# Huber loss on one core: sixteen rows of the first loads sent apart, and new widths for the second and the end tiles

## The chip, the cores and the metric

The kernel runs on one core of a Trainium2 chip. The metric is the device time of one execution in microseconds (us). The time before is the median of three runs. A profile of one execution shows the instructions of each engine and the packets of the sixteen DMA engines that serve the core; VectorE is called DVE in it, ScalarE ACT, SyncE SP.

## The reference

```
diff = pred - target                      # both 8192 x 8192, float32
abs_diff = |diff|
out = 0.5 * diff**2          where abs_diff <= 1
      abs_diff - 0.5         elsewhere
```

Two inputs of 268 MB are read from the chip's memory (HBM) and one output of 268 MB is written.

## The kernel before, in words

The arrays are taken as flat. The 524,288 columns that each of the 128 partitions gets are cut into 37 tiles (`widths`, line 28). A tile is one contiguous stretch of HBM; each partition takes one contiguous run of it, so a load or store of a tile has 128 rows, one per partition. Tile 0 has GAP = 9408 columns, tile 1 has 12,000, tiles 2 to 35 have W = 14,592 each, and the last has 6752.

All of it lives in one buffer `mem` of 3 W + GAP columns. Even and odd tiles alternate between places. `at_b(i)` is where a tile's target is loaded, where the difference is written over it and where the result ends: column 0 for even tiles, W for odd ones. `at_a(i)` is where its pred is loaded, later used for a temporary: 2 W for even tiles, flush to the buffer's end for odd ones. The pred places of neighbouring full tiles overlap by R = W - GAP = 5184 columns; `covered(i)` gives this overlap. Tile i's work does that stretch first (the held piece), so that the next tile's pred can be loaded over it early.

`parts(i)` says in which column ranges a tile is loaded: tile 0 and the last two come in halves, the third from the end in two unequal parts, all others in one. `load(i)` issues for each part the pred and then the target (for the last tile both preds first). All loads and stores are issued by SyncE on one queue, in program order: line 80 in `load`, line 85 in `store`.

`work(i, then)` cuts the parts into pieces (`pieces`, `split`) and runs three steps over each: `subtract` (line 95, DVE: d = a - b; line 96, ACT: absolute value), `square` (line 100, DVE: clip; line 103, ACT: 0.5 x squared) and `combine` (line 107, DVE: the larger of |d| - 0.5 and the square). After the held piece's subtract it calls `then`, which issues the next tile's load.

The order of SyncE's queue is: load(0), load(1), then for each tile store(i - 1), and inside the work of tile i load(i + 1). A pred load waits on the subtract of the held piece that it overwrites. A target load waits on the store of the tile two before, which held its place. A store waits on the last combine of its tile. The waits follow from the data and are put in by the framework.

Of the kernel before, what the change touches and what calls it, by code (L numbers as in the profile page):

```python
# [1 line left out]

# [4 lines left out]


@with_exitstack
def kernel(  # L10
    ctx: ExitStack,
    tc: tile.TileContext,
    pred: bass.AP,
    target: bass.AP,
    out: bass.AP,
):
    nc = tc.nc
    P = 128
    fp32 = mybir.dt.float32
    Alu = mybir.AluOpType  # L20
    Act = mybir.ActivationFunctionType
    SQRT_HALF = 0.70710678118654752

    total = pred.shape[0] * pred.shape[1] // P
    W = 14592
    GAP = 9408
    R = W - GAP
    widths = [GAP, W - R // 2] + [W] * 34
    widths.append(total - sum(widths))
    n = len(widths)  # L30
    starts = [sum(widths[:i]) * P for i in range(n)]

    def block(x, i):
        flat = x.rearrange("r m -> (r m)")
        return flat[starts[i] : starts[i] + P * widths[i]].rearrange("(p m) -> p m", p=P)

    pool = ctx.enter_context(tc.tile_pool(name="memory", bufs=1))
    mem = pool.tile([P, 3 * W + GAP], fp32, name="mem")

    def at_a(i):
        return 3 * W + GAP - widths[i] if i % 2 else 2 * W

    def at_b(i):
        return W if i % 2 else 0

    def covered(i):  # L50

        if i + 1 >= n:
            return (0, 0)
        lo = max(at_a(i), at_a(i + 1))
        hi = min(at_a(i) + widths[i], at_a(i + 1) + widths[i + 1])
        return (lo - at_a(i), hi - at_a(i)) if hi > lo else (0, 0)


    def parts(i):
        w = widths[i]  # L60
        if i == n - 3:
            return [(w - 2 * R, w), (0, w - 2 * R)]
        if i in (0, n - 2, n - 1):
            return halves(w)
        return [(0, w)]

    def halves(w):
        h = w // 32 * 16
        return [(0, h), (h, w)]

    def view(base, lo, hi):
        return mem[:, base + lo : base + hi]

    def load(i):
        order = [(x, part) for part in parts(i) for x in "pt"]
        if i == n - 1:
            order = [(x, part) for x in "pt" for part in parts(i)]
        for x, (lo, hi) in order:
            src, base = (pred, at_a(i)) if x == "p" else (target, at_b(i))
            nc.sync.dma_start(out=view(base, lo, hi), in_=block(src, i)[:, lo:hi])  # L80

    def store(i):
        w = widths[i]
        for lo, hi in halves(w) if i == n - 1 else [(0, w)]:
            nc.sync.dma_start(out=block(out, i)[:, lo:hi], in_=view(at_b(i), lo, hi))

    def split(lo, hi, size):
        k = -((lo - hi) // size)
        edges = [lo + (hi - lo) * j // k // 16 * 16 for j in range(k)] + [hi]
        return list(zip(edges[:-1], edges[1:]))  # L90


    def subtract(i, lo, hi, at):
        a, d = view(at_a(i), lo, hi), view(at_b(i), lo, hi)
        nc.vector.tensor_tensor(out=d, in0=a, in1=d, op=Alu.subtract)  # L95
        nc.scalar.activation(out=d, in_=d, func=Act.Abs)  # L96

    def square(i, lo, hi, at):
        d, t = view(at_b(i), lo, hi), view(at_a(i) + at, 0, hi - lo)
        nc.vector.tensor_scalar(  # L100
            out=t, in0=d, scalar1=-1.0, scalar2=1.0, op0=Alu.max, op1=Alu.min
        )
        nc.scalar.activation(out=t, in_=t, func=Act.Square, scale=SQRT_HALF)  # L103

    def combine(i, lo, hi, at):
        d, t = view(at_b(i), lo, hi), view(at_a(i) + at, 0, hi - lo)
        nc.vector.scalar_tensor_tensor(  # L107
            out=d, in0=d, scalar=-0.5, in1=t, op0=Alu.add, op1=Alu.max
        )

    def pieces(i, lo, hi):


        c0, c1 = covered(i)
        c0, c1 = max(lo, c0), min(hi, c1)
        if c1 <= c0:
            k = -((lo - hi) // (R // 2 if i < n - 1 else R // 4))
            return [], [(i, x, y, x) for x, y in split(lo, hi, -((lo - hi) // k))]
        x, y = (lo, c0) if c0 > lo else (c1, hi)
        m = max(c1 - c0, (y - x) // 32 * 16)  # L120
        rest = [(x, x + m), (x + m, y)] if y > x + m else [(x, y)]
        return [(i, c0, c1, x)], [(i, x, y, x) for x, y in rest]

    def work(i, then):

        todo, held = [], []
        for part in parts(i):
            first, rest = pieces(i, *part)
            todo += first + rest
            held += first  # L130
        mid, end = [], []
        if held:
            subtract(*todo.pop(0))
        then()
        while todo or mid or end or held:
            if todo:
                piece = todo.pop(0)
                subtract(*piece)
                mid.append(piece)
                if len(mid) < 2 and todo:  # L140
                    continue
            if mid:
                piece = mid.pop(0)
                square(*piece)
                end.append(piece)
                if len(end) < 2 and (todo or mid):
                    continue
            combine(*end.pop(0))
            mid += held
            held = []  # L150

    ctx.enter_context(tc.manual_schedule())

    load(0)
    load(1)
    for i in range(n):
        if i > 0:
            store(i - 1)
        work(i, lambda: load(i + 1) if 0 < i < n - 1 else None)
    store(n - 1)  # L160


# [1 line left out]
_INS = ['pred', 'target']  # L164
_OUTS = [((8192, 8192), 'float32')]


# [23 lines left out]
```

## Time and profile before

| What | Value |
|---|---|
| Median of three runs | 1867.21 us (1866.58 to 1867.41) |
| The profiled execution | 1866.7 us |
| Its span, first to last instruction | 1864.9 us |
| DVE busy | 1408.3 us, 76% |
| ACT busy | 912.5 us, 49% |
| Queue of the loads and stores, share of 16 DMA engines | 99.9% |
| HBM read and written | 536.87 MB and 268.44 MB, 432 GB/s over the span |

The page gives each engine's busy time, the packets and bytes of the DMA queues, the costliest groups of instructions and the time from a transfer's issue to its landing. A transfer is spread over several DMA engines and has landed when each of them has set its mark. DMA share is the mean busy share of the sixteen DMA engines; a packet is put into the window in which it starts, so very short windows can show more than 1.

### The profile page before, as it was taken

The numbers are of one execution on the slowest core, as the hardware profiler recorded it, in microseconds if no ns is written. First come the engines' busy times: TensorE is split into PE (matmuls) and PEld (weight loads), VectorE is DVE, ScalarE is ACT, GpSimd is POOL, SyncE is SP. The second block draws the span as 40 slices with busy tenths as digits, with TensorE's granted clock in tenths as the row PEclk, the third lists the DMA queues.
The fourth block names the chain that finished last, engine by engine and source line by source line (L and its number), as shares of the span: only waits on it lengthen the run. The fifth ranks groups of instructions, "written<-read, shape, count | busy, mean of one in ns | idle before, by whom it ended". The sixth has DMA issues, their size and how long they took to land.

```text
span 1864.9 us, 960 instructions
## 1 busy us (share of the span) xinstructions
DVE 1408.3 (76%) x357; ACT 912.5 (49%) x239; POOL 0.2 (0%) x4
## 2 busy tenths in 40 slices
DVE  5677777777788777777778877777777887777986
ACT  3455444444555545444455554544445555454554
POOL 0000000000000000000000000000000000000000
DMA  9999999999999999999999999999999999999999
GB/s 421 418 436 431 436 431 432 437 427 436 438 428 434 439 428 435 438 429 433 438 428 436 438 428 435 438 428 436 438 427 437 436 429 437 435 429 436 428 437 393
DMA packets 17287, 805.37 MB, mean 432 GB/s; under 512 B 1920, under 2 KB 1920, under 8 KB 1920
## 3 DMA queue, kind: packets, MB, share of 16 engines
q1 hardware_dynamic: 17280, 805.31, 99.9%
q14 instruction: 7, 0.06, 0.0%
HBM read 536.87 MB, written 268.44 MB: 432 GB/s over the span
## 4 chain that ended last, share of the span: by engine, by line
DMA 56%; DVE 26%; ACT 13%; issue 4%; another core or an unknown queue 1%; SPq 0%; DVEq 0%
DMA mem<-in_target_dram 32%; DMA out_dram<-mem 24%; DVE mem L107 11%; DVE mem L95 11%; ACT mem L103 8%; ACT mem L96 4%; DVE mem L100 3%; SPq L80 0%; DVEq L95 0%
## 5 line engine op out<-in xcount | busy, mean ns | idle before, releaser
L96 ACT ACTIVATE mem<-mem 128x5184 f32<-128x5184 f32 (+8 forms) x119 | 459.2, 3874 | 756.3 <-DVE mem L95 756.2
L95 DVE TENSOR_TENSOR mem<-mem 128x5184 f32<-128x5184 f32 (+8 forms) x119 | 558.5, 4743 | 336.2 <-DMA mem<-in_target_dram 336.2
L107 DVE SCALAR_TENSOR_TENSOR mem<-mem 128x5184 f32<-128x5184 f32 (+8 forms) x119 | 564.4, 4745 | 74.5 <-ACT mem L103 70.6
L103 ACT ACTIVATE mem<-mem 128x5184 f32<-128x5184 f32 (+8 forms) x119 | 456.7, 3864 | 169.2 <-DVE mem L100 169.2
L100 DVE TENSOR_SCALAR mem<-mem 128x5184 f32<-128x5184 f32 (+8 forms) x119 | 292.0, 2453 | 34.9 <-ACT mem L96 29.9
L96 ACT ACT_TABLE_LOAD x1 | 1.3, 1283 | 14.6 <-DMA mem<-in_target_dram 14.6
L175 POOL MEMSET const-bfloat16-1.0<- 128x1 bf16 x1 | 0.1, 103 | 0.0
L175 POOL MEMSET const-uint8-127<- 128x1 uint8 x1 | 0.1, 102 | 0.0
L175 POOL MEMSET const-float32-0.0<- 128x1 f32 x1 | 0.1, 100 | 0.2 <-issue 0.2
L175 POOL MEMSET const-float32-1.0<- 128x1 f32 x1 | 0.1, 99 | 0.0
## 6 DMA issues: line engine op xcount, KB each, us to landing
out_dram<-mem SPq DMA_DIRECT2D x34, 7296.0 KB, 26.5
mem<-in_pred_dram SPq DMA_DIRECT2D x32, 7296.0 KB, 28.7
mem<-in_target_dram SPq DMA_DIRECT2D x32, 7296.0 KB, 34.4
mem<-in_pred_dram SPq DMA_DIRECT2D x2, 3648.0 KB, 27.6
mem<-in_target_dram SPq DMA_DIRECT2D x2, 3648.0 KB, 25.5
mem<-in_pred_dram SPq DMA_DIRECT2D x1, 6000.0 KB, 36.8
mem<-in_target_dram SPq DMA_DIRECT2D x1, 6000.0 KB, 51.5
out_dram<-mem SPq DMA_DIRECT2D x1, 6000.0 KB, 24.6
```

The lines of the kernel that those rows point to most:

```text
L95: nc.vector.tensor_tensor(out=d, in0=a, in1=d, op=Alu.subtract)
L96: nc.scalar.activation(out=d, in_=d, func=Act.Abs)
L100: nc.vector.tensor_scalar(out=t, in0=d, scalar1=-1.0, scalar2=1.0, op0=Alu.max, op1=Alu.min)
L103: nc.scalar.activation(out=t, in_=t, func=Act.Square, scale=SQRT_HALF)
L107: nc.vector.scalar_tensor_tensor(out=d, in0=d, scalar=-0.5, in1=t, op0=Alu.add, op1=Alu.max)
L175: nc = _bacc.Bacc("TRN2", target_bir_lowering=False, num_devices=1)
```

## The change

The first three transfers of tile 0 (first half of pred, first half of target, second half of pred) are each issued as three: rows 0 to 111, rows 112 to 119 and rows 120 to 127. The fourth (second half of target) and all others keep 128 rows.

Tile 1 gets W = 14,592 columns instead of 12,000. Its load comes in two parts, columns 0 to 2 R = 10,368 and the rest (4224 columns), each with pred and target. Its held piece becomes 5184 columns instead of 2592.

The second tile from the end has 13,056 columns instead of 14,592, still in halves; the last has 5696 instead of 6752. The number of tiles stays 37. The third from the end keeps its width; as its neighbour is narrower, its held piece is 3648 columns instead of 5184, and the rest of that part becomes two pieces.

```diff
-    widths = [GAP, W - R // 2] + [W] * 34
+    widths = [GAP] + [W] * 34 + [13056]
     widths.append(total - sum(widths))
...
     def parts(i):
         w = widths[i]
+        if i == 1:
+            return [(0, 2 * R), (2 * R, w)]
         if i == n - 3:
             return [(w - 2 * R, w), (0, w - 2 * R)]
...
-        for x, (lo, hi) in order:
+        for k, (x, (lo, hi)) in enumerate(order):
             src, base = (pred, at_a(i)) if x == "p" else (target, at_b(i))
-            nc.sync.dma_start(out=view(base, lo, hi), in_=block(src, i)[:, lo:hi])
+
+            apart = i == 0 and k < 3
+            for r0, r1 in [(0, 112), (112, 120), (120, 128)] if apart else [(0, P)]:
+                nc.sync.dma_start(
+                    out=mem[r0:r1, base + lo : base + hi], in_=block(src, i)[r0:r1, lo:hi]
+                )
```

## The prediction

> **What bounds the kernel now.** I read the page first, then the DMA share in windows, then the first and last microseconds of the timeline. From the page, the busy line of the engines and the DMA totals:
>
> ```profile
> DVE 1408.3 (76%) x357; ACT 912.5 (49%) x239; POOL 0.2 (0%) x4
> ...
> DMA packets 17287, 805.37 MB, mean 432 GB/s; under 512 B 1920, under 2 KB 1920, under 8 KB 1920
> ...
> q1 hardware_dynamic: 17280, 805.31, 99.9%
> ```
>
> No compute engine is the bound: VectorE idles 24% of the span, while the one queue keeps the sixteen DMA engines occupied 99.9% of it. Section 6 of the page counts 120 transfers; 120 x 128 rows + 120 x 16 small packets = 17,280. So every row is one packet, never split, and every transfer closes with sixteen marks, one per DMA engine. Next, windows (columns: stretch, length, busy of DVE, ACT and POOL, clock, DMA share, GB/s):
>
> ```profile
> 190.00:1000.00 810.00, 610.79 (x141) 393.84 (x94) 0.00 (x0) 1.00 1.00 433
> 1000.00:1700.00 700.00, 527.78 (x122) 338.85 (x81) 0.00 (x0) 1.00 1.00 434
> ...
> 1858.00:1860.00 2.00, 0.00 (x0) 0.00 (x0) 0.00 (x0) 1.00 1.02 432
> 1860.00:1861.00 1.00, 0.00 (x0) 0.00 (x0) 0.00 (x0) 1.00 0.67 284
> 1861.00:1862.00 1.00, 0.00 (x0) 0.00 (x0) 0.00 (x0) 1.00 0.57 243
> 1862.00:1863.00 1.00, 0.00 (x0) 0.00 (x0) 0.00 (x0) 1.00 0.29 122
> 1863.00:1864.00 1.00, 0.00 (x0) 0.00 (x0) 0.00 (x0) 1.00 0.07 27
> ```
>
> The rate is flat at 433 GB/s, 27.06 per DMA engine; only in the last 4 us do engines run out. The completion marks of the last store say the same: eight at 1860.7 to 1861.4, eight at 1862.7 to 1864.1. The time is therefore that of the slowest of sixteen streams, each fed without a gap. With 50.3 MB per stream at 27.06 GB/s it moves data for 1860 of 1864.9 us, so no removed wait can buy more than a few microseconds; the change acts through how much each stream carries and how fast. Last, the timeline's starts and the end of the first tile:
>
> ```profile
> 0.73 0.37 SPq L80 DMA_DIRECT2D mem<-in_pred_dram  x1
> 1.16 0.42 SPq L80 DMA_DIRECT2D mem<-in_target_dram  x1
> ...
> 25.81 2.61 DVE L95 TENSOR_TENSOR mem<-mem 128x2352 f32<-128x2352 f32 x1 [4.76 <-DMA mem<-in_target_dram]
> ...
> 44.92 0.35 SPq L85 DMA_DIRECT2D out_dram<-mem  x1
> ```
>
> Tile 0 needs 19.2 us from its last load (25.7) to its store.
>
> **The change, part by part.** The sum stands on the profiled execution: 1866.7 us, span 1864.9, last completion mark 1864.1; it lies 0.5 below the median 1867.21.
>
> Bytes: unchanged. Packets: three loads as three pieces keep their 384 rows; tile 1 in two parts adds 256 rows, 16 per engine. Rows of 13,504 bytes still ran at 432 GB/s (1858 to 1860, above) against 433 for 58,368: under 0.1 us per transfer, taken as 0.1.
>
> Issues: six more in load(0) and two more in load(1), each about 0.43 + 0.05 us on SP's queue: 8 x 0.48 = 3.8, so the last of load(1) goes out at 7.9 instead of 4.1 us. The first target piece is out by 2.6 us, and by then every engine holds seven rows of 18,816 bytes, 7 x 0.695 = 4.9 us (18,816 / 27.06). Cover: these rows. Cost nothing; without the cover up to 3.8 us.
>
> The 8-row groups are what counts. No transfer in the trace has fewer than 128 rows, so the price needs bounds. One packet a row means that eight rows occupy at most eight engines, for at least one row's 0.695 us; if one stream had all eight, 5.56. Normally eight rows per engine pass in 5.56 us. With a piece of 112 rows at seven per engine, and the same eight engines taking one row of each group, these eight carry 9 rows per load and the others 7: +0.70 and -0.70 per load, +2.1 and -2.1 us in all. If the groups fell on different engines each time, nothing would move. That is the low end, and it goes below nothing where the eight unburdened ones were the late ones.
>
> The high end asks where the 27.06 GB/s sits. Loads from HBM and stores to HBM run at the same 433, at rows of 13.5 KB as of 58 KB: the limit is one that both directions share, so either the engine itself or its door into the on-chip memory, one sixteenth of the 128 partitions (8 rows of 128) each. [...] In the change they part: the sixteen rows 112 to 127 are two doors' worth if doors lie by neighbours, four if each takes two bunches of four. With four rows behind each other at one door, a group holds its eight engines 4 x 0.695 = 2.78 us, two groups 5.56; per load they then need 4.87 + 5.56 = 10.43 instead of 5.56, +4.87, and over three loads +14.6 us. With eight behind each other it would be +31.
>
> [...]
>
> I take +14.6 for one half of the engines: the rate common to both directions and to all row sizes is nearer to a door than to an engine's handling of packets, which would show in the short rows. Is it given back? A late engine never runs dry: store(0) goes out 19.2 us after tile 0's last load, now 40.3 + 19.2 = 59.5, while the late eight still hold tile 1's rows until 40.3 + 34.5 = 74.8. Only the early eight run dry (from about 58), and every later step waits for all sixteen marks. So the delay runs through to the last store.
>
> Tile 1, full: its first part (10,368 columns) lands 24.5 us after tile 0, the held 5,184-column subtract takes 5.6, and load(2)'s pred is issued at 40.3 + 30.1 = 70.4, before the late engines end at 74.8. The second part, behind which SyncE queues nothing, lands before VectorE reaches it. Cost nothing: the cover is the queued rows, 4.4 us of it (before: issued 58.2, queue until 65.7).
>
> End tiles: the last tile's compute shrinks from 19.2 us (1834.8 to 1854.0) to 19.2 x 5696/6752 = 16.2; the rows queued behind its first target part from 4.0 + 17.3 + 4.0 = 25.3 to 3.4 + 15.4 + 3.4 = 22.2. Slack 6.0 against 6.1: nothing. Last targets wait for store(34), covered by pred rows of 6.7 instead of 8.0 us: still covered for the engines that end last.
>
> Sum: if the eight loaded engines were the early ones, 1860.7 + 14.6 = 1875.3; if the late ones, 1864.1 + 14.6 = 1878.7. Plus 2.6 to the execution's end and 0.5 to the median: 1878.4 to 1881.8, forecast 1880.0. Collisions inside the 112-row pieces, whose seven rows per engine no longer match doors, could add up to one 2.78 per load (8 us): 1888.
>
> **Rivals.** *The engine is the limit, not the door* (0.26): only +2.1 and -2.1. Loaded ones early before: 1861.4 + 2.1 = 1863.5 = 0.6 less, 1866.6. Loaded ones late: 1864.1 + 2.1, 1869.3. For it: the equal rate; against: the same rate suits a door. Not slower than this measurement can tell, which is about 0.2% or 3.7 us.
>
> *Nothing moves* (0.10): pieces go to engines by partition, rows 112 to 127 to the same engines as before, and 1867 stays. [...]
>
> *Faster by breaking the lockstep* (0.07). All sixteen engines turn from loads to the first store together, and the page's issues show a price:
>
> ```profile
> mem<-in_pred_dram SPq DMA_DIRECT2D x1, 6000.0 KB, 36.8
> mem<-in_target_dram SPq DMA_DIRECT2D x1, 6000.0 KB, 51.5
> ```
>
> Issued at 3.1 and 3.6, they land at 39.9 and 55.1: 15.2 us for the second, 14.2 (from 25.7) for the first: 1.0 lost at the turn. Later turns leave the 3.4 us between first and last mark. If the shift spared all engines all of it, 1867.2 - 3.4 - 1.0 = 1862.8. It decides if the two halves are shifted without either gaining work, which the row count speaks against.
>
> *Dry queue* (0.04): a transfer early or at the end is issued too late for the late engines too; 4 to 6 us, 1872.
>
> **How the numbers follow.** Door 0.53, engine 0.26, nothing 0.10, faster 0.07, dry 0.04. Slower 0.53 + 0.04 = 0.57, same 0.36, faster 0.07. Cases of both kinds hold much, so the range reaches from 1865.0 (below the engine case's 1866.6, with the 1.0 turn spared) to 1888.0; the forecast case alone is 1876 to 1888.
>
> **What would show it.** Right: tile 0's last subtract starts near 40 instead of 25.8, the first store near 59 instead of 44.9, DMA share well under 1 before 60 us, then 433 GB/s, and the last completion marks more than 10 us apart. Engine case: that subtract at about 27.9, spread 2 to 6 us. Nothing moves: 25.8 again. If the first store comes as late as forecast but the span does not grow, the late engines got their time back, and the step "never runs dry, never given back" fails.

## The result, and the profile after

The changed kernel takes 1889.8 us (median of four runs, 1889.1 to 1890.6) against 1867.1 for the kernel before: 22.7 us more, ratio 1.0123 with a 95% interval of 1.011 to 1.0135. Slower was forecast, but with +12.9 us; 1889.8 lies just above the range's 1888.

From the page of the changed kernel, the busy line and the DMA totals:

```profile
DVE 1408.7 (75%) x363; ACT 913.1 (48%) x243; POOL 0.2 (0%) x4
...
DMA packets 17624, 805.38 MB, mean 427 GB/s; under 512 B 2000, under 2 KB 2000, under 8 KB 2000
...
q1 hardware_dynamic: 17616, 805.31, 99.8%
```

Compute and bytes are the same and the queue still fills 99.8% of the span, yet the mean rate is 427 instead of 432 GB/s. The small packets tell how the new pieces were spread: 122 transfers with sixteen marks are 1952, and the 48 left are eight for each of the six 8-row groups. Taken as one mark per engine, each group went to eight.

Windows of the first 50 us (stretch, length, busy of DVE, ACT and POOL, clock, DMA share, GB/s), the changed kernel:

```profile
0.00:10.00 10.00, 0.00 (x0) 0.00 (x0) 0.20 (x4) 1.00 0.93 239
10.00:20.00 10.00, 0.00 (x0) 0.00 (x0) 0.00 (x0) 1.00 0.95 192
20.00:30.00 10.00, 0.00 (x0) 0.01 (x1) 0.00 (x0) 1.00 1.03 188
30.00:40.00 10.00, 6.42 (x3) 7.65 (x4) 0.00 (x0) 1.00 1.01 209
40.00:50.00 10.00, 1.73 (x1) 0.00 (x0) 0.00 (x0) 1.00 0.99 397
50.00:60.00 10.00, 10.00 (x6) 6.97 (x4) 0.00 (x0) 1.00 1.01 435
...
190.00:1000.00 810.00, 616.72 (x143) 399.99 (x96) 0.00 (x0) 1.00 1.00 434
1000.00:1700.00 700.00, 528.51 (x122) 342.25 (x82) 0.00 (x0) 1.00 1.00 434
```

Nearly the whole loss is here. For 40 us all engines count as busy (share 0.93 to 1.03) while they move 188 to 239 GB/s; from 50 us on the rate is 434 to 435 again, against 433 to 434 before. The first 50 us in one window, before and after:

```profile
0.00:50.00 50.00, 25.50 (x12) 18.26 (x9) 0.20 (x4) 1.00 0.99 420
```

```profile
0.00:50.00 50.00, 8.15 (x4) 7.66 (x4) 0.20 (x4) 1.00 0.98 245
```

The timeline gives the size of the loss, by the same two instructions that the prediction showed:

```profile
48.27 2.61 DVE L102 TENSOR_TENSOR mem<-mem 128x2352 f32<-128x2352 f32 x1 [11.82 <-DMA mem<-in_target_dram]
...
67.38 0.35 SPq L92 DMA_DIRECT2D out_dram<-mem  x1
```

Tile 0's third subtract starts at 48.27 instead of 25.81, 22.5 us later; the first store goes out 22.5 later; the span grows by 22.4 (1864.9 to 1887.3). That the last two numbers agree so closely is chance. Against the profile of the kernel with the new widths alone (below), which has the same tiles, the stores go out 22.5 us late at first, 19.0 at the thirteenth and 20.7 at the last, and the span is 22.0 longer. So most of what is lost in the first loads stays lost; some 3 us come back and are lost again later, and no run shows by what.

### The profile page after: what moved, and what is told of

Read it like the earlier page. It is cut to its first block, busy times and chain, and to the rows that moved or that the text cites. A ratio compares the mean times of both kernels' runs of the same rounds, so it can differ in the third digit from the quotient of the medians.

```text
span 1887.3 us, 987 instructions
## 1 busy us (share of the span) xinstructions
DVE 1408.7 (75%) x363; ACT 913.1 (48%) x243; POOL 0.2 (0%) x4
## 3 DMA queue, kind: packets, MB, share of 16 engines
q1 hardware_dynamic: 17616, 805.31, 99.8%
## 4 chain that ended last, share of the span: by engine, by line
DMA 58%; DVE 25%; ACT 12%; issue 4%; SPq 0%; DVEq 0%
DMA mem<-in_target_dram 34%; DMA out_dram<-mem 24%; DVE mem L114 11%; DVE mem L102 11%; ACT mem L110 8%; ACT mem L103 4%; DVE mem L107 3%; SPq L85 0%; DVEq L102 0%
## 5 line engine op out<-in xcount | busy, mean ns | idle before, releaser
L103 ACT ACTIVATE mem<-mem 128x5184 f32<-128x5184 f32 (+8 forms) x121 | 459.6, 3813 | 762.4 <-DVE mem L102 762.3
L114 DVE SCALAR_TENSOR_TENSOR mem<-mem 128x5184 f32<-128x5184 f32 (+7 forms) x121 | 564.7, 4669 | 73.1 <-ACT mem L110 69.2
L110 ACT ACTIVATE mem<-mem 128x5184 f32<-128x5184 f32 (+7 forms) x121 | 457.2, 3803 | 169.0 <-DVE mem L107 169.0
L107 DVE TENSOR_SCALAR mem<-mem 128x5184 f32<-128x5184 f32 (+7 forms) x121 | 292.3, 2416 | 33.2 <-ACT mem L103 28.2
```

Source lines behind the costliest of these rows:

```text
L107: nc.vector.tensor_scalar(out=t, in0=d, scalar1=-1.0, scalar2=1.0, op0=Alu.max, op1=Alu.min)
L114: nc.vector.scalar_tensor_tensor(out=d, in0=d, scalar=-0.5, in1=t, op0=Alu.add, op1=Alu.max)
```

## The experiments

Each kernel was timed in alternation with the kernel before; its median (1867.0 to 1867.4) is the base of the differences. The doors of the expectations, and the bunches of four partitions that share one, are the author's assumption: no trace records a door, or which engine took a packet. What a run shows is the rows that a load fills, its time and its rate.

**The rows alone, the widths alone.**

```diff
-    widths = [GAP] + [W] * 34 + [13056]        # rows alone: this and parts(1) as before
+    widths = [GAP, W - R // 2] + [W] * 34
-            apart = i == 0 and k < 3           # widths alone: only this
+            apart = False
```

> The rows apart, the widths and parts as before. Doors theory (bunches of neighbouring partitions share a path of 27 GB/s, so the pieces of 112 and 8 rows stall engines behind each other): nearly the whole loss, 1888 to 1890 us. If the widths and parts carried part of the loss: clearly under that, 1870 to 1885.

> All loads with 128 rows, the new widths and parts kept. Doors theory: the loss is gone, 1867 us, within 2 us either way. If the widths and parts carried part of the loss: 1870 us or more.

Rows alone: 1891.2 us, ratio 1.0134 (1.012 to 1.0149), as the changed kernel within the intervals and just above the expected 1888 to 1890. Widths alone: 1866.96, ratio 0.9998 (0.9989 to 1.0007). The rows carry all of it; the full second tile, its two parts and the end tiles cost and bring nothing that can be measured.

**As many transfers, by columns.** The three loads in three pieces each, all of 128 rows.

```diff
-            for r0, r1 in [(0, 112), (112, 120), (120, 128)] if apart else [(0, P)]:
+            cols = [(lo, lo + 1568), (lo + 1568, lo + 3136), (lo + 3136, hi)] if apart else [(lo, hi)]
+            for c0, c1 in cols:
```

> The same three loads each in three transfers, but cut by columns, all with 128 rows: as many transfers, issues and waits on SyncE's queue as in the change. Doors theory: nothing but 48 more packets per engine, 1867 to 1868 us. Rival (the number of transfers, their issues and the waits between them cost the time): 1880 us or more.

1867.07 us, ratio 1.0001 (0.9992 to 1.001). The number of transfers, their issues and their waits are not the cost. With the rows kernel beside it, that leaves the rows that a transfer has.

**Halves, and sixteen together.** Two splits meant to leave every engine eight rows per load.

```diff
-            for r0, r1 in [(0, 112), (112, 120), (120, 128)] if apart else [(0, P)]:
+            for r0, r1 in [(0, 64), (64, 128)] if apart else [(0, P)]:       # halves
+            for r0, r1 in [(0, 112), (112, 128)] if apart else [(0, P)]:     # sixteen together
```

> The same three loads as rows 0 to 63 and 64 to 127: every engine has eight rows per load as before and no engine is favoured. Doors theory: 64 neighbouring rows reach only half the doors, two engines at each, so a load takes 11.1 instead of 5.6 us, +16 us over three loads, 1880 to 1885. Rival (the loss comes from transfers that only eight engines carry, nine rows against seven): nothing, 1867 us.

> As the change, but rows 112 to 127 go as one transfer, one row on each of sixteen engines: every engine has eight rows per load. Doors theory: the piece of 16 rows reaches four doors, 2.8 us for all engines instead of 0.7, and the piece of 112 rows keeps its collisions (8 instead of 4.9 us as in the changed kernel): 11 us per load, +16 us, 1880 to 1886. Rival (uneven load, nine rows against seven, makes the loss): back to 1867 us.

Halves: 1884.9, +17.8 (ratio 1.0092, 1.0078 to 1.0106). Sixteen together: 1881.2, +14.1 (1.0078, 1.0063 to 1.0093). By the marks no engine is favoured in either: both pages have 2000 small packets for 125 transfers, sixteen marks each. So the loss needs no uneven load, and 64 neighbouring rows pass at about half of the 433 GB/s (211, below). The difference of 8.6 us between sixteen together and the changed kernel is what cutting sixteen rows into eights adds. Windows of the halves:

```profile
10.00:20.00 10.00, 0.00 (x0) 0.00 (x0) 0.00 (x0) 1.00 1.00 211
20.00:30.00 10.00, 3.49 (x2) 2.13 (x2) 0.00 (x0) 1.00 1.01 211
```

With all sixteen engines occupied (share 1.00 and 1.01), 211 GB/s is about eight times the 27 GB/s that one engine has before (216): the figure that the doors theory gives for half of the doors.

**One load apart.**

```diff
-            apart = i == 0 and k < 3
+            apart = i == 0 and k < 1
```

> Only the first load of tile 0 goes apart. Doors theory: a third of the loss or a little more, since later loads only add their own collisions: +6 to +9 us, 1873 to 1876. If the loss came once (at the start, or from losing step once): the full +22 us, 1889.

1877.96, +10.8 us: above the expected +6 to +9. Tile 0's third subtract starts 7.5 us late (33.33), a third of the changed kernel's 22.5 as expected. The rest comes near the end: against the widths kernel the first store is 7.6 us late, the thirtieth 7.6, the last 9.3, and the span is 10.3 longer. From what, no run shows.

**The pieces by themselves.** Six extra loads ahead of all others in the kernel before, into columns that are free until tile 1's load; what they bring is not used.

```diff
+    for j in range(6):
+        at = (W if j < 3 else 2 * W + GAP) + j % 3 * 4704
+        nc.sync.dma_start(out=mem[112:120, at : at + 4704], in_=block(pred, 0)[112:120, 0:4704])
     load(0)
# spread:        out=mem[64:96:4, ...]     low rows:      out=mem[0:8, ...]
# 112 rows:      mem[0:112, ...], block(pred, 0)[0:112]
# every second:  mem[0:128:2, ...], block(pred, 0)[0:64]
```

> Kernel before, with six extra loads ahead of all others, each of 8 rows of 18,816 bytes into rows 112 to 119 of columns that are free until tile 1's load (work added, nothing used). Doors theory: two doors for eight rows, 2.8 us each on eight engines, 16.7 us: 1880 to 1884. Rival (each engine just carries one row more, 0.70 us): 4.2 us on eight engines, 1868 to 1872, the same as with rows spread.

> The same six extra loads from the same rows of HBM, but into every fourth of rows 64 to 95, eight rows in eight bunches of four. Doors theory: eight doors, 0.70 us each, 4.2 us on eight engines: 1868 to 1872 us. Rival, HBM side (the eight rows are slow to read): as slow as with neighbouring rows, 1880 or more.

> As the kernel with six extra loads of 8 neighbouring rows, from the same rows of HBM, but into rows 0 to 7 instead of 112 to 119. There, the eight engines without an extra row were slowed as much as the eight with one. If they were slowed because the flooded doors lie in their own half of the partitions: here they run free, eight engines at 54 GB/s for the extra rows and the other eight at their full 216 until they have run through their queued loads, and four streams meet at a door instead of five, 2.8 us each, +15 to +17 us, 1882 to 1884. If the engines are tied to each other whatever the door (common order of the rows): again a rate of about 85 GB/s with all engines occupied, and +19 to +20 us, 1887.

| Six extra loads of | us | more | each |
|---|---|---|---|
| 8 neighbours, rows 112 to 119 | 1886.9 | 19.7 | 3.29 |
| 8 neighbours, rows 0 to 7 | 1883.9 | 16.9 | 2.81 |
| 8 rows spread by four, 64 to 92 | 1873.4 | 6.2 | 1.04 |
| 64 rows, every second | 1884.4 | 16.9 | 2.82 |
| 112 rows, 0 to 111 | 1913.6 | 46.1 | 7.69 |

The last column is the whole difference divided by six. The first three read the same eight rows of HBM; only the partitions that they fill differ. So the price is on the on-chip side. Windows of rows 112 to 119, of rows 0 to 7, and of the spread rows:

```profile
8.00:12.00 4.00, 0.00 (x0) 0.00 (x0) 0.00 (x0) 1.00 0.93 80
12.00:16.00 4.00, 0.00 (x0) 0.00 (x0) 0.00 (x0) 1.00 0.99 85
```

```profile
8.00:12.00 4.00, 0.00 (x0) 0.00 (x0) 0.00 (x0) 1.00 1.02 108
12.00:16.00 4.00, 0.00 (x0) 0.00 (x0) 0.00 (x0) 1.00 1.10 118
```

```profile
0.00:4.00 4.00, 0.00 (x0) 0.00 (x0) 0.20 (x4) 1.00 0.24 75
4.00:8.00 4.00, 0.00 (x0) 0.00 (x0) 0.00 (x0) 1.00 0.77 202
8.00:12.00 4.00, 0.00 (x0) 0.00 (x0) 0.00 (x0) 1.00 0.94 339
12.00:16.00 4.00, 0.00 (x0) 0.00 (x0) 0.00 (x0) 1.00 1.01 433
```

With neighbours a fifth to a quarter of 433 GB/s is left, with share 0.93 to 1.10. In the packets of the traces, one of 18,816 bytes takes 3.47 us for rows 112 to 119 and 2.80 for rows 0 to 7 (medians from 8 to 16 us): 5.0 and 4.0 times the 0.70 of a packet in the kernel before. By the author's doors that would be five and four streams at one door; the traces show the times alone, not what shares a door or which engines took the pieces.

The last expectation came out half each way. The time, 1883.9, was the one expected for four streams at a door (1882 to 1884). The rate was nearer to the one expected for tied engines (about 85 GB/s): every packet from 8 to 16 us took 2.75 to 2.86 us, with all sixteen engines busy at 108 to 118 GB/s together, where 54 + 216 = 270 was expected if the other eight ran free. So no engine, with an extra row or without one, passed a packet at the 0.70 us of the kernel before; what held them to one pace, the runs do not show.

The spread rows cost 1.04 each instead of the 0.70 expected, and 1873.4 lies above the 1868 to 1872. Part of that is no price of the rows: SyncE issued the first full load at 4.92 us instead of 0.73, and until then most engines had little to do. The share in the first two windows is 0.24 and 0.77, against these in the kernel before:

```profile
0.00:4.00 4.00, 0.00 (x0) 0.00 (x0) 0.20 (x4) 1.00 0.60 198
4.00:8.00 4.00, 0.00 (x0) 0.00 (x0) 0.00 (x0) 1.00 1.02 433
```

That is an estimated 4 x (0.36 + 0.25) = 2.4 us of the 6.2; the rest is 0.6 for each load, near the 0.70.

> Kernel before, with six extra loads ahead of all others, each of rows 0 to 111 (18,816 bytes a row, into columns free until tile 1's load; work added, nothing used): a piece of 112 rows measured by itself. By rows per engine, as the prediction's sum had it: 7 x 0.695 = 4.9 us each, +29 us, 1896. Doors theory with engines that take seven neighbouring rows each: they fall out of line with the bunches of four, 7 to 8.2 us each, +42 to +49 us, 1909 to 1916.

> Kernel before, with six extra loads ahead of all others, each of 64 rows into every second partition from 0 to 126, so that all sixteen doors get four rows. If pieces are dealt to engines by the partition's own door: 4 x 0.695 = 2.8 us each, +17 us, 1884. If engines take consecutive rows of the piece, two of them meet at each door all the time although all doors have work: 5.6 us each, +33 us, 1900.

Windows of the 112-row loads, then of every second row:

```profile
8.00:12.00 4.00, 0.00 (x0) 0.00 (x0) 0.00 (x0) 1.00 1.07 259
12.00:16.00 4.00, 0.00 (x0) 0.00 (x0) 0.00 (x0) 1.00 0.91 259
```

```profile
8.00:12.00 4.00, 0.00 (x0) 0.00 (x0) 0.00 (x0) 1.00 0.99 423
12.00:16.00 4.00, 0.00 (x0) 0.00 (x0) 0.00 (x0) 1.00 0.99 419
```

A piece of 112 neighbouring rows costs 7.69 us, not the 4.9 of seven rows per engine and more than the 5.56 of a whole 128-row load. That engines take seven neighbours each and so fall out of line with the bunches of four was the author's reason for expecting 7 to 8.2; the size agrees, the assignment of rows was not seen. The kernel with every second row speaks against it as a general rule: it took 1884.4, the 1884 expected if pieces are dealt by the partition's own door, and not the 1900 expected of consecutive rows. So why 112 rows cost more than 5.56 stays open. Half of the rows, every second one, run at nearly the full rate, 419 to 423 GB/s, against the 211 of 64 neighbours.

**Stores.**

```diff
+            for r0, r1 in [(0, 64), (64, 128)] if i < 2 else [(0, P)]:      # in store(i)
```

> Kernel before, with the stores of tiles 0 and 1 cut into rows 0 to 63 and 64 to 127. If reading the on-chip memory goes through the same doors: each store takes double, +11.1 and +14.2 us, 1890 to 1893. If only writing has doors: nothing, 1867.

1888.65, +21.2 us (ratio 1.0115, 1.01 to 1.013). Stores of 64 neighbouring rows pay as loads do, which is what the author expected if reading the on-chip memory goes through the same doors. That the rows are the cause is argued rather than shown: no run stored spread rows, so the HBM side and the number of transfers are not ruled out. The time lies below the expected 1890 to 1893, 4 us under the 25.3 of two fully doubled stores; which part was saved was not followed up.

## Why the prediction was right or wrong

- **What bounds it, and that delay is not given back: right in the main.** 22.5 us are lost by tile 0's third subtract and the span is 22.4 longer. In between the stores are only 19.0 us late, so the close agreement is luck.
- **Issues, packets, tile 1, end tiles at nothing: right**, by the columns and the widths kernels (1.0001 and 0.9998). The issue times were wrong. The last of load(1) went out at 29.92 us, not at 7.9: SyncE issued eight transfers by 3.65 us and then waited for earlier ones to land, the ninth leaving at 12.17. In the columns kernel, too, the last left only at 14.41. Neither cost time: the columns kernel loses nothing, and in the changed kernel the share of the first 50 us is 0.98, against 0.99 before.
- **The door's price, not the engine's: right.** The engine rival allowed 1866.6 to 1869.3. Eight neighbours cost 2.81 to 3.29 us each by themselves, against 2.78 in the sum and 0.70 for an engine-bound row. The 2.78 is four rows behind each other at one door, on the same eight engines for each group, and no run shows that term; what the runs show in its place is eight marks per group and packets of 2.80 us (rows 0 to 7) and 3.47 us (rows 112 to 119) instead of 0.70, with all sixteen engines busy (share 0.93 to 1.10).
- **The 112-row piece at 7 x 0.695 = 4.9 us: wrong, and the step that failed.** It took the engine's view for this piece and the door's view for the groups; by the door's view, which no trace shows, most doors keep their eight rows in it, so that 5.56 was the least. By itself the piece costs 7.69, 2.8 us more; over three loads 8.4. Why it is that much over 5.56 stays open. The kernel with sixteen together agrees: 14.1 / 3 + 5.56 - 2.78 = 7.5 for the same piece, if its sixteen rows cost 2.78. Put into the sum, 14.6 + 8.4 = 23.0, against 22.7 measured. That this is so close is partly luck: with the 3.29 that rows 112 to 119 cost by themselves, in place of 2.78, it would be 26.1. The text had these collisions, up to 8 us, but only in the upper edge of the range and not in the forecast.
- **"The others carry 7 rows, 0.70 less per load", and early engines that run dry from about 58 us: wrong.** With eight extra rows in rows 0 to 7, no packet from 8 to 16 us took less than 2.75 us on any engine, so none ran at the 0.70 a row that the sum gave to those without an extra one. No eight engines ran 10 us ahead here either: DMA share stays near 1, and the last store's marks lie 6 us apart (1880.5 to 1886.5), not over 10.
- **"DMA share well under 1 before 60 us" as the sign: wrong.** An engine whose packet is held up counts as busy (share 0.93 to 1.03 at 188 to 239 GB/s). The sign was in the GB/s.
- **The marks before.** Seven lie at 1860.7 to 1861.4 and nine at 1862.7 to 1864.1, not eight and eight, and the sum took 1860.7 for the early engines where their last mark is 1861.4. That is 0.7 us and changes nothing in the account.
- **The rivals.** Nothing moves: the time rules it out (1889.8, not 1867). Lockstep broken: no gain is seen; the rate after 50 us is the same 434 GB/s. Dry queue: the share of 0.98 over the first 50 us leaves no room for it.

## What to carry to other kernels

Where the DMA engines bound a kernel as they do here (99.9% of the span), cut a transfer by columns (three loads in nine pieces cost nothing, ratio 1.0001), or, if by rows, into rows that lie spread (tried here only as extra loads: 64 rows, every second, ran at 419 to 423 GB/s); 64 neighbouring rows halved the rate (211 GB/s) and eight neighbours cut it to a fifth or a quarter (80 to 118). Read GB/s beside the busy share: sixteen busy engines moved 80 GB/s here. None of the versions tried beats the kernel before; the best, the new widths alone and the columns, equal it.

## What the runs showed of the hardware that was not expected

Eight rows loaded into neighbouring partitions slowed every packet, not theirs alone: with rows 0 to 7 filled, all sixteen engines together moved 108 to 118 GB/s, at 2.75 to 2.86 us for every packet from 8 to 16 us instead of 0.70. What held them to one pace is open. And a 112-row load takes longer (7.69 us) than a 128-row load of the same columns (5.56 at 433 GB/s), though it moves an eighth less.
